# Scan spacing of twelve steps, and a reordered first job, in a one-core hybrid decoder layer

## The chip, the core and the metric

The kernel runs on one core of a Trainium2 chip. TensorE (PE in the profile) multiplies matrices, VectorE (DVE) and ScalarE (ACT) do elementwise work, GpSimd (POOL) some elementwise work and DMA issues, and SyncE (SP) issues DMAs. The metric is device time in microseconds, the median of several executions. The three runs shown lie within 0.45 us of each other; the profile shows one execution.

## The reference

One layer with parallel head groups is applied to a prompt (16 learned meta tokens and 256 prompt tokens) and to a sample group of 8 sequences of 4 tokens: T = 304 columns in all. D_MODEL is 2048, the feed-forward width 5632, and all data are fp32.

```python
xp = _layernorm(jnp.concatenate([meta, x_prompt], axis=1), ln0_g, ln0_b)
xs = _layernorm(x_sample, ln0_g, ln0_b)
...
proj = x @ w_in                       # q, zf, v, g (8 heads x 128 each), gate_b, gate_c, xin
...
# per head and chunk of 64 tokens
a = jnp.einsum('bhtk,bhsk->bhts', qc * jnp.exp(b - b_mid), kc * jnp.exp(b_mid - b))
o = einsum(where(causal, a, 0), vc) + einsum(qc * jnp.exp(b), S)
S = jnp.exp(b_last) * S + einsum(kc * jnp.exp(b_last - b), vc)
...
o = o * lax.rsqrt(jnp.mean(jnp.square(o), axis=-1, keepdims=True) + RMS_EPS)
o_a = o * gnorm_g * jax.nn.silu(g)
y_b = gate_b * conv(gate_c * xin)
mix = jnp.concatenate([o_a, y_b], axis=-1) @ w_o
h = _layernorm(ALPHA * x + mix, ln1_g, ln1_b)
ff = (jax.nn.silu(h @ w_gate) * (h @ w_up)) @ w_down
out = _layernorm(ALPHA * h + ff, ln2_g, ln2_b)
```

The scan state and the last convolution inputs are outputs too.

## The kernel before, in words

**Products.** Activations stand transposed, features on the 128 partitions and tokens along the free dimension. A product of fp32 precision is made of three: both operands are split into a high part rounded to the PE's fp32r type and a low rest (`hi`, `lo` of a weight, `mh`, `ml` or `xh`, `xl` of an activation), and hi*high, hi*low and lo*high are accumulated. Weights come in pieces of 4 blocks of 128 rows by 256 columns (`raw`, 512 KB, issued by SP). ACT casts a piece to `hi` and DVE subtracts to get `lo`, a few pieces ahead of PE.

**Jobs and steps.** The work is a row of jobs (`run_job`): a job makes 256 output rows in two PSUM banks from all blocks k of the contraction, six products to a block. After each block `tick()` is called: this is one step. Everything else is written as generators in named lanes (`side`), and each lane goes on to its next `yield` at a step; `yield n` skips n steps. So the order in which the small work stands in the program is counted in steps of six products. A list scheduler may then move instructions of an engine, except those issued through `vec`, `act`, `pool`, `pe` and `sync`, which keep their written order. Each engine runs its own queue strictly in order (PE's weight loads apart).

**Jobs in order.** Four jobs (z, v, q, gate) for each of four pairs of heads, with three convolution jobs each (cb, xb, gbb) between and after them, then eight jobs for w_o, then the feed-forward in two halves (gate, up, down).

**Scans.** `scan_head(h, ...)` runs eight times in one lane, one after the other. It transposes v (`vtb`) at its first step; DVE and ACT form the decays (`c`, `b`, `el`, `eb`), the scaled keys `kp` and `kd`; POOL multiplies the old state (`sn`, line 641); 15 steps after `vtb` PE transposes the keys (`ktb`, lines 661 to 663), two steps later it makes the scores (`ab`), and 15 steps after `ktb` the output (`ob`). Then it starts the lane `gated` for this head and ends with `yield GAP`, so the next head's scan starts GAP steps after `ob`. `gated` squares `ob` four steps after it, lets PE average (`nb`) two steps later, and about four steps after that begins eight DVE operations of 128x288 (`c<-nb`, `w<-eq`, ... `ml<-eq,mh`), the last of which makes this head's rows of the mixer input. Heads 2p and 2p+1 wait for the four jobs of pair p; the first scan also waits for step DEFER = 96.

**The first job.** The input rows are in three tiles `xts` (128, 128 and 48 rows, 2048 columns), loaded in four column chunks c of 512. `centre` subtracts a rough mean from a chunk, `turn(k)` transposes block k on PE (`xT`), `settle(k)` makes `mh` (ACT) and `ml` (DVE) of it. The first job (`zb`, `first_rhs`) runs on these centred but unnormalised rows; the LayerNorm's mean and scale are applied afterwards to its output. The statistics of tiles 0 and 1 come from `bn_stats` on DVE; those of tile 2 from two passes of ACT over all 2048 columns (`row_sums`, `junk`). `rstd_tok` turns them into `xr` and `xn`, PE broadcasts those into `rb`, and after `rb` the transposes `pb` and `bufT` of parameter rows stand, then the job vT. `idle_product` multiplies the identity with itself, at the front, to no end but PE activity. `lower_bounds` forms `loglb` and its kin from `pb`.

```python
        yield GAP                                    # last line of scan_head
...
            if k in BN_AT:
                b = BN_AT.index(k)
                row_stats(b % 2, b // 2)
            if k in (9, 10):
                next(sums)
```

Of the kernel before, what the change touches and what calls it, by code (L numbers as in the profile page):

```python
# [9 lines left out]
F32 = mybir.dt.float32  # L10
# [3 lines left out]
ALU = mybir.AluOpType  # L14

P = 128
# [25 lines left out]
DEFER = 96  # L42
BN_AT = (1, 3, 5, 6, 7, 9, 10, 11)
WARM = 3
LAG = 4
GAP = 8
NX = 7
# [16 lines left out]
def hybrid_step(ctx: ExitStack, tc: tile.TileContext, io):  # L64
# [166 lines left out]

    load_rows(pool, prow0, 0, ("ln0_g",))
    ident = const.tile([P, P], F32, name="ident")
    make_identity(nc, ident)

    def pcol(name, i):
# [106 lines left out]
    with s0x:  # L343
# [3 lines left out]
        bns = [x0p.tile([P, NXC, 6], F32, name=f"bn{i}") for i in range(2)]  # L347
        s2t = x0p.tile([P, 3], F32, name="s2t")
        prows = x0p.tile([NP1, P], F32, name="prows")
# [31 lines left out]
        def idle_product(n):  # L381
            pe.matmul(warm[:, : n * P], ident, ident.unsqueeze(1).broadcast_to([P, n, P]), start=True, stop=True)

        for _ in range(WARM):
            idle_product(4)
        idle_product(2)

# [8 lines left out]
        def centre(i, c, eng):  # L396
            n = rows[i]
            x, m = xts[i][:n, c * XC : (c + 1) * XC], cen[:n, i : i + 1]
            if eng is act:
                eng.activation(out=x, in_=x, func=AF.Identity, bias=m)  # L400
            else:
                eng.tensor_scalar(out=x, in0=x, scalar1=m, scalar2=None, op0=ALU.add)
# [15 lines left out]

        def row_sums():

            n = rows[2]
            x2, m2, s2 = xts[2][:n], mv[:n, 2], s2t[:n]
            junk = x0p.tile([n, D], F32, name="junk")
            act.activation(out=junk, in_=x2, func=AF.Identity, accum_out=s2[:, 0:1])
            vec.tensor_scalar(out=m2[:, 0:1], in0=s2[:, 0:1], scalar1=1.0 / D, scalar2=None, op0=ALU.mult)
            vec.tensor_scalar(out=s2[:, 2:3], in0=s2[:, 0:1], scalar1=-1.0 / D, scalar2=None, op0=ALU.mult)
            yield
            act.activation(out=junk, in_=x2, func=AF.Square, bias=s2[:, 2:3], accum_out=s2[:, 1:2])
            vec.tensor_scalar(out=m2[:, 1:2], in0=s2[:, 1:2], scalar1=1.0 / D, scalar2=None, op0=ALU.mult)
            yield  # L430

        row_centre(0)
        centre(0, 0, vec)
        row_centre(2)
        centre(2, 0, act)
        row_centre(1)
        centre(1, 0, vec)
        pb = bank("pb", "main")
        pe.transpose(pb[:, :NP0], prow0, ident[:NP0, :NP0])
        vec.tensor_copy(out=pvec[:, :NP0], in_=pb[:, :NP0])  # L440
        turn(0)
        turn(1)
        idle_product(2)
        settle(0)
# [5 lines left out]
        for _ in first_split:  # L450
            pass
        sums = row_sums()
        stats = []
# [5 lines left out]
        def first_rhs(k):  # L459
            c, i = divmod(k, 4)  # L460
            if i == 0:
                for j in (2, 3):
                    turn(k + j)
                for j in (2, 3):
                    settle(k + j)
                if c + 1 < NXC:
                    for j, eng in ((2, act), (0, vec), (1, act if c else vec)):
                        centre(j, c + 1, eng)
                if k == 0:
                    load_rows(pool, prows, NP0, ("b_f", "lb_param", "gnorm_g", "ln1_g", "ln1_b"))  # L470
                    pool.dma_start(out=crows, in_=io["conv_w"][0].rearrange("j (a b) -> (j a) b", b=P))
                    pool.dma_start(out=brow, in_=io["state_conv"][0].rearrange("b j c -> (b j) c"))
            if i == 2:
                split_next()
                if k + 2 < NB:
                    for j in (2, 3):
                        turn(k + j)
                    for j in (2, 3):
                        settle(k + j)
            if k in BN_AT:  # L480
                b = BN_AT.index(k)
                row_stats(b % 2, b // 2)
            if k in (9, 10):
                next(sums)
            if k == 13:
                for j in range(2):
                    vec.bn_aggr(out=mv[:, j], in_=bns[j])
                stats.extend(rstd_tok(x0p, mv, P, 3, "x"))
            return mixh[:, k], mixl[:, k]

        first_job = run_job(first_rhs, T + 2, "zb", pe)

        rb = [bank("rb") for _ in range(2)]
        for b, src in zip(rb, stats):
            for i in range(3):
                pe.matmul(b[:, i * P : i * P + rows[i]], src[:, i : i + 1].broadcast_to([P, P]), ident[:, : rows[i]],
                          start=True, stop=True)
        pb = bank("pb")
# [6 lines left out]
        for i in range(H):  # L505
            nc.tensor.transpose(bb_[:, i * 2 * DB : (i + 1) * 2 * DB], brow[:, i * P : (i + 1) * P], ident[: 2 * DB, : 2 * DB])
        nc.vector.tensor_copy(out=bufT, in_=bb_[:, : H * 2 * DB].rearrange("p (i b j) -> p i b j", b=DB, j=2))

    s2 = ExitStack()
# [794 lines left out]
```

## Time and profile before

| | |
|---|---|
| median of 3 runs | 1414.9 us (1414.69 to 1415.14) |
| profiled execution, its own time | 1415.39 us |
| its span in the trace | 1413.7 us |
| PE busy | 1388.5 us (98%) |
| DVE, ACT, POOL busy | 868.1, 604.7, 106.4 us |
| mean granted PE clock | 0.994 |
| weights and all else read from HBM | 222.34 MB |

The time of an execution has 1.7 us outside the span. PE is busy for nearly the whole span, so what is not PE's own work is found by listing where PE idles, not by the shares of the other engines. The granted clock is the share of the full PE clock that the chip allows in a stretch.

### The profile page before, as it was taken

The page shows a single profiled execution, that of the slowest core. Times are in us where ns is not written, and L with a number is a line of the kernel's source. Part 1 is how long each engine was busy: PE and PEld are TensorE (multiplying, and loading weights), DVE is VectorE, ACT ScalarE, POOL GpSimd, SP SyncE. Part 2 cuts the span into 40 slices and gives each one's busy share as a digit, 9 for nine tenths or more (in the row PEclk, how much of TensorE's full clock was granted, in tenths as well). Part 3 has the DMA queues.
Part 4 walks back from the last instruction along what each step waited for, and adds up shares of the span by engine and source line. Part 5 has one row for each costly group of instructions (what it writes and reads, how often), then busy time and mean ns, then how long its engine had stood idle before and what let it go on. Part 6 is the DMA issues. An engine that isn't in the chain of part 4 may idle for free.

```text
span 1413.7 us, 25159 instructions
## 1 busy us (share of the span) xinstructions
PE 1388.5 (98%) x10333; PEld 1369.3 (97%) x10333; DVE 868.1 (61%) x1431; ACT 604.7 (43%) x880; POOL 106.4 (8%) x165
## 2 busy tenths in 40 slices
PE   8999999999999999999999999999999999999996
PEld 6999999999999999999999999999999999999995
DVE  7996877786676787966444444443444444465544
ACT  6775445545443444434333333333333333343330
POOL 4000111111010332000000000000000000020000
PEclk9999999999999999999999999999999999999997
DMA  7746555455545555555555545556555555565541
GB/s 213 229 150 186 152 165 166 136 158 167 167 144 162 158 158 164 167 170 165 167 167 165 165 149 164 165 166 179 168 167 168 167 164 164 165 195 165 156 128 68
DMA packets 224660, 231.14 MB, mean 164 GB/s; under 512 B 7964, under 2 KB 219784, under 8 KB 224410
## 3 DMA queue, kind: packets, MB, share of 16 engines
q1 hardware_dynamic: 220688, 218.03, 50.5%
q0 software_dynamic: 3552, 11.12, 2.7%
q8 instruction: 81, 1.33, 0.4%
q10 hardware_dynamic: 304, 0.37, 0.1%
q14 instruction: 35, 0.29, 0.1%
HBM read 222.34 MB, written 7.15 MB: 162 GB/s over the span
## 4 chain that ended last, share of the span: by engine, by line
PE 90%; DVE 7%; ACT 2%; issue 1%; POOL 0%; DVEq 0%; POOLq 0%; ACTq 0%
PE u L201 7%; PE g L201 7%; PE wd L203 7%; PE g L202 7%; PE u L202 7%; PE wd L202 7%; PE g L203 7%; PE u L203 7%; PE wd L201 7%; PE wo L202 2%; PE wo L201 2%; PE wo L203 2%; DVE lo L79 1%; PE sg L201 1%; PE vT L203 1%; PE sg L202 1%
## 5 line engine op out<-in xcount | busy, mean ns | idle before, releaser
L79 DVE TENSOR_TENSOR lo<-raw,hi 128x1024 fp32r<-128x1024 f32 (+1 forms) x408 | 498.6, 1224 | 468.5 <-ACT hi L78 467.8
L78 ACT CAST hi<-raw 128x1024 fp32r<-128x1024 f32 (+1 forms) x408 | 420.7, 1032 | 614.7 <-PE u L202 162.6
L202 PE MATMUL wd<-al,hi 128*128 128x288 f32 x704 | 207.9, 295 | 0.0
L201 PE MATMUL wd<-ah,hi 128*128 128x288 f32 x704 | 207.8, 295 | 0.0
L203 PE MATMUL wd<-ah,lo 128*128 128x288 f32 x704 | 207.8, 295 | 0.0
L201 PE MATMUL g<-ygh,hi 128*128 128x288 f32 (+1 forms) x452 | 134.0, 296 | 0.0
L202 PE MATMUL g<-ygl,hi 128*128 128x288 f32 (+1 forms) x452 | 134.0, 296 | 0.0
L202 PE MATMUL u<-ygl,hi 128*128 128x288 f32 (+1 forms) x452 | 133.9, 296 | 0.0
L201 PE MATMUL u<-ygh,hi 128*128 128x288 f32 (+1 forms) x452 | 133.8, 296 | 0.0
L203 PE MATMUL g<-ygh,lo 128*128 128x288 f32 (+1 forms) x452 | 133.6, 296 | 0.0
L203 PE MATMUL u<-ygh,lo 128*128 128x288 f32 (+1 forms) x452 | 133.6, 296 | 0.0
L202 PEld LDWEIGHTS wd<-al,hi 128*128 128x128 f32 x704 | 132.3, 188 | 0.0
L203 PEld LDWEIGHTS wd<-ah,lo 128*128 128x128 f32 x704 | 132.2, 188 | 0.0
L201 PEld LDWEIGHTS wd<-ah,hi 128*128 128x128 f32 x704 | 132.1, 188 | 0.1
L203 PEld LDWEIGHTS u<-ygh,lo 128*128 128x128 f32 x452 | 85.4, 189 | 0.0
L203 PEld LDWEIGHTS g<-ygh,lo 128*128 128x128 f32 x452 | 85.3, 189 | 0.0
L201 PEld LDWEIGHTS g<-ygh,hi 128*128 128x128 f32 x452 | 85.3, 189 | 0.1
L202 PEld LDWEIGHTS g<-ygl,hi 128*128 128x128 f32 x452 | 85.3, 189 | 0.1
L201 PEld LDWEIGHTS u<-ygh,hi 128*128 128x128 f32 x452 | 85.3, 189 | 0.0
L202 PEld LDWEIGHTS u<-ygl,hi 128*128 128x128 f32 x452 | 85.3, 189 | 0.0
L203 PE MATMUL wo<-mh,lo 128*128 128x288 f32 x256 | 75.8, 296 | 0.0
L202 PE MATMUL wo<-ml,hi 128*128 128x288 f32 x256 | 75.8, 296 | 0.0
(461 smaller groups left out, 3206.1 us busy)
## 6 DMA issues: line engine op xcount, KB each, us to landing
raw<-in_w_in SPq DMA_DIRECT2D x111, 512.0 KB, 3.7
raw<-in_w_gate SPq DMA_DIRECT2D x88, 512.0 KB, 3.6
raw<-in_w_up SPq DMA_DIRECT2D x88, 512.0 KB, 3.6
raw<-in_w_down SPq DMA_DIRECT2D x79, 512.0 KB, 3.6
raw<-in_w_o SPq DMA_DIRECT2D x32, 512.0 KB, 3.7
s<-in_state_hgrn POOLq DMA_DIRECT2D x8, 512.0 KB, 5.7
out<-sn POOLq DMA_DIRECT2D x8, 512.0 KB, 4.6
raw<-in_w_down SPq DMA_DIRECT2D x15, 256.0 KB, 2.8
```

The lines of the kernel that those rows point to most:

```text
L78: a.copy(out=hi, in_=src)
L79: v.tensor_tensor(out=lo, in0=src, in1=hi.bitcast(F32), op=ALU.subtract)
L201: eng.matmul(o, hi[:, i % kb, cs], xh, start=(i == 0), stop=False)
L202: eng.matmul(o, hi[:, i % kb, cs], xl, start=False, stop=False)
L203: eng.matmul(o, lo[:, i % kb, cs], xh, start=False, stop=(i == nk - 1))
```

## The change

GAP goes from 8 to 12: each scan starts twelve steps after the `ob` of the one before. In the first job the second tile's statistics are gathered while it is centred: the ACT centring of tile 2 also writes its sum for the chunk (`accum_out`), four ACT passes over 512 columns add the squares (`row_squares` at k = 5, 7, 9, 11), and `row_moments` combines these on DVE at k = 13; the two passes over 2048 columns go. Chunks 2 and 3 of tile 0 are centred by POOL instead of DVE. The eight `bn_stats` move to later k. Of the idle products, 3 of 512 columns and 2 of 256 become 3 of 512; the one small transpose `pb` of the front moves between them. On POOL the DMA of `ln0_g` comes after the identity instead of before it, and the parameter rows' DMAs come at k = 4 instead of k = 0, behind POOL's first centring. The transposes `pb` and `bufT` behind the first job, and `lower_bounds`, are written ahead of `rb`.

```diff
--- before.py
+++ after.py
@@ -40,10 +40,11 @@
 NXC = 4
 NRAW = 8
 DEFER = 96
-BN_AT = (1, 3, 5, 6, 7, 9, 10, 11)
-WARM = 3
+BN_AT = (3, 5, 6, 7, 9, 10, 11, 12)
+SQ_AT = (5, 7, 9, 11)
+WARM = 2
 LAG = 4
-GAP = 8
+GAP = 12
 NX = 7
 RAW = 4
 ORDER = (("head", 0), ("head", 1), ("conv", 0), ("head", 2), ("conv", 1), ("head", 3), ("conv", 2), ("conv", 3))
@@ -229,9 +230,9 @@
             off[name] = row
             row += n
 
-    load_rows(pool, prow0, 0, ("ln0_g",))
     ident = const.tile([P, P], F32, name="ident")
     make_identity(nc, ident)
+    load_rows(pool, prow0, 0, ("ln0_g",))
 
     def pcol(name, i):
         return pvec[:, off[name] + i : off[name] + i + 1]
@@ -345,7 +346,7 @@
 
         mv = x0p.tile([P, 3, 2], F32, name="mv")
         bns = [x0p.tile([P, NXC, 6], F32, name=f"bn{i}") for i in range(2)]
-        s2t = x0p.tile([P, 3], F32, name="s2t")
+        s2t = x0p.tile([P, 2, NXC], F32, name="s2t")
         prows = x0p.tile([NP1, P], F32, name="prows")
         crows = x0p.tile([3 * H, P], F32, name="crows")
         xts = [x0p.tile([P, D], F32, name=f"xt{i}") for i in range(3)]
@@ -383,7 +384,9 @@
 
         for _ in range(WARM):
             idle_product(4)
-        idle_product(2)
+        pb = bank("pb", "main")
+        pe.transpose(pb[:, :NP0], prow0, ident[:NP0, :NP0])
+        idle_product(4)
 
 
         cen = x0p.tile([P, 3], F32, name="cen")
@@ -397,7 +400,7 @@
             n = rows[i]
             x, m = xts[i][:n, c * XC : (c + 1) * XC], cen[:n, i : i + 1]
             if eng is act:
-                eng.activation(out=x, in_=x, func=AF.Identity, bias=m)
+                eng.activation(out=x, in_=x, func=AF.Identity, bias=m, **({"accum_out": s2t[:n, 0, c : c + 1]} if i == 2 else {}))
             else:
                 eng.tensor_scalar(out=x, in0=x, scalar1=m, scalar2=None, op0=ALU.add)
 
@@ -416,31 +419,32 @@
             vec.scalar_tensor_tensor(out=mixl[:, k, :T], in0=b, scalar=g, in1=mixh[:, k, :T].bitcast(F32),
                                      op0=ALU.mult, op1=ALU.subtract)
 
-        def row_sums():
-
+        junk = x0p.tile([rows[2], XC], F32, name="junk")
+
+        def row_squares(c):
             n = rows[2]
-            x2, m2, s2 = xts[2][:n], mv[:n, 2], s2t[:n]
-            junk = x0p.tile([n, D], F32, name="junk")
-            act.activation(out=junk, in_=x2, func=AF.Identity, accum_out=s2[:, 0:1])
-            vec.tensor_scalar(out=m2[:, 0:1], in0=s2[:, 0:1], scalar1=1.0 / D, scalar2=None, op0=ALU.mult)
-            vec.tensor_scalar(out=s2[:, 2:3], in0=s2[:, 0:1], scalar1=-1.0 / D, scalar2=None, op0=ALU.mult)
-            yield
-            act.activation(out=junk, in_=x2, func=AF.Square, bias=s2[:, 2:3], accum_out=s2[:, 1:2])
-            vec.tensor_scalar(out=m2[:, 1:2], in0=s2[:, 1:2], scalar1=1.0 / D, scalar2=None, op0=ALU.mult)
-            yield
+            act.activation(out=junk, in_=xts[2][:n, c * XC : (c + 1) * XC], func=AF.Square, accum_out=s2t[:n, 1, c : c + 1])
+
+        def row_moments():
+
+            for i in range(2):
+                vec.bn_aggr(out=mv[:, i], in_=bns[i])
+            n = rows[2]
+            m2, sums = mv[:n, 2], x0p.tile([P, 3], F32, name="sums")[:n]
+            vec.tensor_reduce(out=sums[:, :2], in_=s2t[:n], op=ALU.add, axis=mybir.AxisListType.X)
+            vec.tensor_scalar(out=m2, in0=sums[:, :2], scalar1=1.0 / D, scalar2=None, op0=ALU.mult)
+            vec.tensor_scalar(out=sums[:, 2:], in0=m2[:, 0:1], scalar1=-1.0, scalar2=None, op0=ALU.mult)
+            vec.scalar_tensor_tensor(out=m2[:, 1:2], in0=m2[:, 0:1], scalar=sums[:, 2:], in1=m2[:, 1:2], op0=ALU.mult, op1=ALU.add)
 
         row_centre(0)
         centre(0, 0, vec)
         row_centre(2)
         centre(2, 0, act)
+        vec.tensor_copy(out=pvec[:, :NP0], in_=pb[:, :NP0])
         row_centre(1)
         centre(1, 0, vec)
-        pb = bank("pb", "main")
-        pe.transpose(pb[:, :NP0], prow0, ident[:NP0, :NP0])
-        vec.tensor_copy(out=pvec[:, :NP0], in_=pb[:, :NP0])
         turn(0)
         turn(1)
-        idle_product(2)
         settle(0)
         gb0 = pvec[:, :NP0].rearrange("p (a b) -> p b a", b=NB)
         split(gb0, mixh[:, :, T:], mixl[:, :, T:], vec, act)
@@ -449,7 +453,6 @@
         settle(1)
         for _ in first_split:
             pass
-        sums = row_sums()
         stats = []
 
         def row_stats(i, c):
@@ -464,9 +467,9 @@
                 for j in (2, 3):
                     settle(k + j)
                 if c + 1 < NXC:
-                    for j, eng in ((2, act), (0, vec), (1, act if c else vec)):
+                    for j, eng in ((2, act), (0, pool), (1, act)) if c else ((2, act), (0, vec), (1, vec)):
                         centre(j, c + 1, eng)
-                if k == 0:
+                if k == 4:
                     load_rows(pool, prows, NP0, ("b_f", "lb_param", "gnorm_g", "ln1_g", "ln1_b"))
                     pool.dma_start(out=crows, in_=io["conv_w"][0].rearrange("j (a b) -> (j a) b", b=P))
                     pool.dma_start(out=brow, in_=io["state_conv"][0].rearrange("b j c -> (b j) c"))
@@ -480,21 +483,14 @@
             if k in BN_AT:
                 b = BN_AT.index(k)
                 row_stats(b % 2, b // 2)
-            if k in (9, 10):
-                next(sums)
+            if k in SQ_AT:
+                row_squares(SQ_AT.index(k))
             if k == 13:
-                for j in range(2):
-                    vec.bn_aggr(out=mv[:, j], in_=bns[j])
+                row_moments()
                 stats.extend(rstd_tok(x0p, mv, P, 3, "x"))
             return mixh[:, k], mixl[:, k]
 
         first_job = run_job(first_rhs, T + 2, "zb", pe)
-
-        rb = [bank("rb") for _ in range(2)]
-        for b, src in zip(rb, stats):
-            for i in range(3):
-                pe.matmul(b[:, i * P : i * P + rows[i]], src[:, i : i + 1].broadcast_to([P, P]), ident[:, : rows[i]],
-                          start=True, stop=True)
         pb = bank("pb")
         nc.tensor.transpose(pb[:, :NP1], prows, ident[:NP1, :NP1])
         nc.tensor.transpose(pb[:, P : P + 3 * H], crows, ident[: 3 * H, : 3 * H])
@@ -505,6 +501,12 @@
         for i in range(H):
             nc.tensor.transpose(bb_[:, i * 2 * DB : (i + 1) * 2 * DB], brow[:, i * P : (i + 1) * P], ident[: 2 * DB, : 2 * DB])
         nc.vector.tensor_copy(out=bufT, in_=bb_[:, : H * 2 * DB].rearrange("p (i b j) -> p i b j", b=DB, j=2))
+
+        rb = [bank("rb") for _ in range(2)]
+        for b, src in zip(rb, stats):
+            for i in range(3):
+                pe.matmul(b[:, i * P : i * P + rows[i]], src[:, i : i + 1].broadcast_to([P, P]), ident[:, : rows[i]],
+                          start=True, stop=True)
 
     s2 = ExitStack()
     sp = s2.enter_context(tc.tile_pool(name="sp", bufs=1))
```

What this does to the queues is shown at three places.

PE, the start of the program, before (`warm` is an idle product, `xt_110`, `xt_112`, `xt_111` are the tiles 0, 2 and 1):

```order
L60 MATMUL warm<-ident 128x512 x3
L60 MATMUL warm<-ident 128x256
L60 MATMUL pb<-ident,prow_70 128x32
L60 MATMUL xT<-ident,xt_110 128x128
L60 MATMUL xT<-ident,xt_112 128x48
L60 MATMUL xT<-ident,xt_111 128x128
```

and in the changed kernel:

```order
L61 MATMUL warm<-ident 128x512 x2
L61 MATMUL pb<-ident,prow_70 128x32
L61 MATMUL warm<-ident 128x512
L61 MATMUL xT<-ident,xt_110 128x128
L61 MATMUL xT<-ident,xt_112 128x48
L61 MATMUL xT<-ident,xt_111 128x128
```

The small transpose now stands between the idle products, and one idle product less lies ahead of the first `xT`; the 256-column one that followed six of the `xT` is gone as well.

DVE, the end of the first job's statistics, before (`bn`, `mv`: statistics; `xv`, `xt`, `xr`, `xn` here: variance, temporary, scale and shift of the rows):

```order
L60 BN_AGGR mv<-bn_105 128x2
L60 BN_AGGR mv<-bn_106 128x2
L60 TENSOR_SCALAR xv<-mv 128x3
L60 TENSOR_TENSOR xt<-xr 128x3
L60 TENSOR_TENSOR xt<-xt,xv 128x3
L60 TENSOR_SCALAR xt<-xt 128x3
L60 TENSOR_TENSOR xr<-xr,xt 128x3
L60 SCALAR_TENSOR_TENSOR xn<-mv,xr 128x3
L60 TENSOR_TENSOR lo<-raw,hi 128x1024
L501 COPY pvec<-pb 128x64
```

and in the changed kernel, from just behind the first `bn_aggr` to the variance `xv`; eight more rows follow up to `xr`, four of them (`es`, `loglb`, `nloglb`, `logom`) of `lower_bounds`:

```order
L497 COPY pvec<-pb 128x64
L61 BN_AGGR mv<-bn_106 128x2
L61 TENSOR_REDUCE sums<-s2t 48x2
L498 COPY cvec<-pb 128x24
L61 TENSOR_SCALAR mv<-sums 48x2
L299 TENSOR_TENSOR lmx<-pvec 128x8
L503 COPY bufT<-bufT 128x128
L61 TENSOR_SCALAR sums<-mv 48x1
L301 TENSOR_TENSOR dd<-pvec,lmx 128x8
L302 TENSOR_TENSOR dd<-pvec,lmx 128x8
L61 SCALAR_TENSOR_TENSOR mv<-mv,sums 48x1
L61 TENSOR_SCALAR xv<-mv 128x3
```

The parameter copies and the lower bounds, which stood behind `xn`, are now mixed into the chain that ends in `xr`; a last `bn_stats` also stands behind the last `ml` where none stood.

DVE, the fourth gate and the fifth scan (head 4), before (`c<-nb`, `w<-eq`, `eq<-...`: the gate of head 3; `vt`, `vbd`, `c<-z`, `k`: the scan of head 4; `lo`: weight pieces):

```order
L742 TENSOR_SCALAR c<-nb 128x288
L589 COPY vt<-vtb 128x256
L79 TENSOR_TENSOR lo<-raw,hi 128x1024
L314 TENSOR_TENSOR w_3195<-eq 128x288
L315 TENSOR_TENSOR w_3195<-w_3195,c 128x288
L604 TENSOR_TENSOR vbd<-vsb,bmask 128x1024
L585 SCALAR_TENSOR_TENSOR c<-z,w_3157 128x304
L316 TENSOR_SCALAR w_3195<-w_3195 128x288
L586 TENSOR_SCALAR c<-c,logom 128x304
L317 TENSOR_TENSOR eq<-eq,w_3195 128x288
L594 TENSOR_TENSOR k<-c,z 128x304
L751 TENSOR_TENSOR eq<-ob,eq 128x288
```

and in the changed kernel:

```order
L744 TENSOR_SCALAR c<-nb 128x288
L315 TENSOR_TENSOR w_3275<-eq 128x288
L316 TENSOR_TENSOR w_3275<-w_3275,c 128x288
L317 TENSOR_SCALAR w_3275<-w_3275 128x288
L80 TENSOR_TENSOR lo<-raw,hi 128x1024
L318 TENSOR_TENSOR eq<-eq,w_3275 128x288
L587 SCALAR_TENSOR_TENSOR c<-z,w_3289 128x304
L753 TENSOR_TENSOR eq<-ob,eq 128x288
L588 TENSOR_SCALAR c<-c,logom 128x304
L754 TENSOR_TENSOR eq<-eq,sg 128x288
L591 COPY vt<-vtb 128x256
L596 TENSOR_TENSOR k<-c,z 128x304
```

The copy `vt`, which cannot run before PE has transposed v, stood one row behind the gate's first row and now stands behind nearly all of the gate. From `w<-eq` to the last `kd` row there are two `lo` rows in this scan before and three now.

## Prediction

> **What bounds the kernel now.** I read the page's first lines, then a table of stages, then what PE waited for, then the timeline at the largest wait. First the page:
>
> ```profile
> span 1413.7 us, 25159 instructions
> PE 1388.5 (98%) x10333; PEld 1369.3 (97%) x10333; DVE 868.1 (61%) x1431; ACT 604.7 (43%) x880; POOL 106.4 (8%) x165
> ```
>
> PE is idle for 25.2 us in all (1413.7 - 1388.5). The stages say where. The columns are the stretch, its length, busy time of PE, of PE's weight loads, DVE, ACT, POOL, then the granted clock, the DMA share and GB/s:
>
> ```profile
> 0.00:10.36 10.36, 7.76 (x24) 3.88 (x24) 6.30 (x15) 3.83 (x8) 8.16 (x32) 1.00 0.83 219
> 10.36:34.50 24.14, 21.32 (x155) 19.73 (x155) 20.57 (x48) 17.58 (x31) 7.46 (x25) 1.00 0.77 211
> ...
> 100.00:420.00 320.00, 311.85 (x2333) 302.81 (x2332) 242.54 (x504) 156.84 (x276) 40.39 (x46) 0.99 0.53 160
> 420.00:1390.00 970.00, 970.00 (x7302) 969.06 (x7301) 522.23 (x701) 373.16 (x464) 45.90 (x56) 1.00 0.53 162
> 1390.00:1413.70 23.70, 12.18 (x57) 8.68 (x56) 12.16 (x37) 1.22 (x4) 0.00 (x0) 0.69 0.29 100
> ```
>
> From 420 to 1390 us PE never idles: 7302 products take 970.00 us, 0.1328 us each, so a step of six is 0.80 us. The change touches the first 34.5 us (PE idle for 2.60 + 2.82 us) and the scans, where PE idles for 320.00 - 311.85 = 8.15 us. Next, what PE waited for from 100 to 560 us (total, times, longest):
>
> ```profile
> PE ktb L661 <- DVE kp L630: 5.5, 5, 2.1
> PE ktb L662 <- DVE kd L638: 1.7, 5, 1.0
> PE ab L668 <- DVE eq L643: 0.9, 1, 0.9
> ```
>
> All 8.1 us are waits of the transposes of keys (and one score product) for DVE. The largest, in head 4, on the timeline (start, duration; idle before in brackets):
>
> ```profile
> 252.11 0.45 DVE L742 TENSOR_SCALAR c<-nb 128x288 f32<-128x288 f32 x1
> 252.96 0.27 PE L570 MATMUL vtb<-ident,vT 128*16 128x128 f32 x1
> 253.27 0.42 DVE L589 COPY vt<-vtb 128x256 f32<-128x256 f32 x1 [0.71 <-PE vtb L570]
> ...
> 264.38 2.10 POOL L641 TENSOR_TENSOR sn<-s,eb 128x1024 f32<-128x1024 f32 x1 [21.80 <-ACT eb L612]
> 264.62 1.91 DVE L622 TENSOR_TENSOR w<-b 128x32 f32<-128x32 f32 x1
> 267.31 0.28 DVE L630 TENSOR_TENSOR kp<-kp,eb 128x128 f32<-128x128 f32 x1
> ...
> 267.65 0.44 PE L661 MATMUL ktb<-ident,kp 128*128 128x128 f32 x2 [2.08 <-DVE kp L630]
> ```
>
> DVE runs without a break from 253.27 to kp's end at 267.59, and PE wants kp at 267.65 - 2.08 = 265.57, which is 12.6 us (fifteen steps) behind `vtb`. In that time DVE must do the gate of head 3 as well. The 1.91 us row is an oddity: the row ahead of it in the trace, of the same 128x32 shape, takes 0.19. It starts under POOL's 2.10 us `sn` and ends with it; one DVE row does so in each of the eight scans.
>
> The wait has an echo in the clock:
>
> ```profile
> 262.10:265.50 3.40, 3.40 (x26) 3.23 (x24) 3.40 (x10) 1.85 (x3) 1.12 (x1) 1.00 0.83 250
> 265.50:269.00 3.50, 1.42 (x12) 1.33 (x12) 3.50 (x14) 2.28 (x6) 0.98 (x1) 0.99 0.14 47
> 269.00:272.40 3.40, 3.40 (x17) 3.40 (x17) 2.48 (x5) 1.39 (x4) 0.00 (x0) 0.50 0.27 70
> 272.40:275.80 3.40, 3.40 (x29) 2.82 (x29) 1.53 (x5) 0.25 (x1) 0.54 (x1) 1.00 0.80 236
> 227.00:230.40 3.40, 1.91 (x14) 1.42 (x13) 3.40 (x13) 1.91 (x7) 1.27 (x1) 1.00 0.50 154
> ```
>
> After the 2.08 us gap the clock was 0.50 for 3.4 us, and 17 products ran where 26 and 29 ran on either side: half of 3.4, 1.7 us, were lost. The last row is head 3, where PE idled for 1.49 us (3.40 - 1.91) and the clock stayed at 1.00.
>
> **The change, part by part.**
>
> *GAP.* Four steps more between `ob` and the next `vtb` are 4 x 0.80 = 3.19 us. The gate's start is tied to its own `ob`, so `c<-nb`, now 0.85 us ahead of `vtb` (252.96 - 252.11), will come about 4.0 ahead. The quoted order shows what that does: between `c<-nb` and `vt` stand six more gate rows, one `lo` and two scan rows, some 5.3 us, so `vt` runs about 1.3 us behind `vtb` (0.31 now). Behind `vt`, up to kp, are left one gate row and the scan's own, with two `lo`; by start-to-start times in the trace these are 9.9 us with the 1.73 us that `sn` costs. So kp is ready 1.3 + 9.9 = 11.2 us behind `vtb`, against 12.6: 1.4 us early instead of 2.1 late. What speaks against a full gain is the count of `lo` rows from `w<-eq` to `kd`: 2, 3, 2, 2, 2 before in heads 2, 3, 4, 5, 7, and 4, 3, 3, 3, 3 after. Their group from 100 to 420 us (busy time, mean ns of one, idle time before them):
>
> ```profile
> L79 DVE TENSOR_TENSOR lo<-raw,hi 128x1024 fp32r<-128x1024 f32 x83 | 101.0, 1222 | 50.4 <-ACT hi L78 50.0
> ```
>
> One is 1.22, or 1.15 from start to start, and may itself wait for ACT's `hi`. I leave 1.0 us of the 8.15 standing (bounds 0 and 5.15, one `lo` in each of the five heads: 5 x 1.15 = 5.75, less what they have in hand; I take the low side because the margin just worked out already holds its extra `lo`): **-7.15**. Behind it nothing is late: six gaps of 3.19 do not add up, since every second head waits for its pair's jobs too; by the order head 7's `vtb` stands only 23 of PE's rows, about four steps, later. The last row of its gate and the first use of the mixer input now:
>
> ```profile
> 438.58 0.45 DVE L79 TENSOR_TENSOR ml<-eq,mh 128x288 fp32r<-128x288 f32 x1
> ...
> L201 PEld LDWEIGHTS wo<-mh,hi x256: 187/188/193, 443.1 to 546.3; 128*128 128x128 f32 x128
> ```
>
> 439.03 + 3.19 = 442.2, still ahead of 443.1.
>
> *The clock.* Without a gap over 2 us the stretch at 269 goes: **-1.7** (0 if a gap like that survives).
>
> *`sn`* stays and blocks one DVE row of a scan as now. The Trainium skill, page "SBUF — State Buffer", section "Who interferes with whom", says that a DVE instruction with two SBUF inputs contends with a GpSimd one that reads SBUF, and that the first to issue locks the shared port pair for its whole length. The trace agrees (1.91 us beside 2.10). By that rule POOL's two new centrings could each hold a DVE `ml` or `lo` for their full length, up to twice 1.05 us (half of `sn`'s length for half its columns), and not free DVE by the 0.96 us worked out below; the first job would be up to 1.1 us worse.
>
> *The first job.* Its rows:
>
> ```profile
> 1.32 0.64 POOL L60 DMA_DIRECT2D prow<-in_ln_g  x1 [0.80 <-POOLq L1292]
> 2.60 5.01 PE L60 MATMUL warm<-ident 128*128 128x512 f32 x8 [2.60 <-POOL ident masks.py:199]
> 8.89 0.60 PE L60 MATMUL warm<-ident 128*128 128x256 f32 x2
> 12.17 1.05 ACT L60 CAST hi<-raw 128x1024 fp32r<-128x1024 f32 x1
> 21.69 1.33 ACT L60 ACTIVATE xt<-xt,cen 48x512 f32<-48x512 f32 x2
> 22.92 1.90 ACT L60 ACTIVATE junk<-xt 48x2048 f32<-48x2048 f32 x1
> 23.15 0.48 DVE L60 TENSOR_SCALAR xt<-xt,cen 128x512 f32<-128x512 f32 x1
> 26.55 2.01 ACT L60 ACTIVATE junk<-xt,s2t 48x2048 f32<-48x2048 f32 x1
> 28.75 0.67 DVE L60 BATCH_NORM_STATS2 bn<-xt 128x6 f32<-128x512 f32 x1
> 30.23 0.37 DVE L60 BATCH_NORM_AGGREGATE mv<-bn 128x2 f32<-128x24 f32 x2
> 31.91 0.16 DVE L60 TENSOR_TENSOR xr<-xr,xt 128x3 f32<-128x3 f32 x1
> 32.22 0.84 PE L60 MATMUL rb<-ident,xr 128*128 128x128 f32 x6 [0.46 <-DVE xr L60]
> 33.66 0.27 PE L499 MATMUL pb<-ident,prows 64*128 64x64 f32 x1
> 34.51 0.41 PE L201 MATMUL vT<-mh,hi 128*128 128x306 f32 x1
> ```
>
> Front: the identity comes 0.64 earlier (the issue at 1.32 goes behind it), and of the idle products 0.60 us fall away. That would be worth 0 to 1.24, but the next thing PE needs is a weight's `hi`, which starts at 12.17 whatever PE does; I keep 0.45, the third nearest the row that ends last. Shorter idle work costs nothing while the clock is 1.00, as here from 10 us on.
>
> ACT: the passes of 1.90 and 2.01 become four of 512 columns at 0.67 (half of the 21.69 row, `accum_out` free), so 1.2 us less on the engine that is busy 12.45 of 13.51 us between 15.94 and 29.45:
>
> ```profile
> 15.94:29.45 13.51, 12.07 (x88) 11.29 (x86) 11.28 (x23) 12.45 (x20) 2.50 (x5) 1.00 0.88 252
> ```
>
> I take 0.9 of it (0 to 1.2), since some of ACT's order is fixed by landings. POOL's two centrings free 2 x 0.48 on DVE, which is not the later engine there: 0 (bounds -0.96 and +1.1). The parameter rows' DMAs move on POOL's queue behind its first centring, to k = 4 of 16, and `pb` wants them at about 30: hidden by eleven blocks of the job. So the last `ml` ends near 30.23 + 0.07 - 1.35 = 28.95.
>
> Behind it DVE now has a `bn_stats` (0.67), two aggregates (0.37), and about fourteen small rows, six of them parameter copies and lower bounds, where the trace has 1.77 us from the last `ml` to `xr`'s end. At 0.15 to 0.2 each: 0.67 + 0.37 + 2.8 is about 3.9 us, so `rb` near 33.0 against 32.22 (+0.8). But `pb` and `bufT`, which took PE 0.85 us (33.66 to 34.51) between `rb` and vT, are done in the wait ahead of `rb`. vT: 34.51 + 0.8 - 0.85, that is **0.0** (bounds -2.0, if the tail overlaps the last products, and +1.0, at 0.25 a row).
>
> **Sum.** 1415.39 - 7.15 - 1.7 + 0.0 = 1406.5. The profiled execution is 0.5 above the median of 1414.9, so **1406.0**. Nothing after 420 us changes.
>
> **Rivals.** A change of 0.2% (2.8 us) is about what can be told from none; faster means below 1412.1.
>
> A (as summed): 1406.0, chance 0.46.
>
> B: as A, but the gap ahead of `rb` sets off a half-clock stretch. PE has only `pb` and `bufT` between the first job's end near 29.5 and `rb` at 33.0, idling for about 2.4 us against 0.46 now. For it: 2.08 us did so in head 4. Against it: 1.49 did not, and the small transposes break the gap. Price 1.7: 1407.7, chance 0.26. By the Trainium skill, page "TensorE: Matmul & The Clock Gate", section "Why this matters for your kernels", only gaps over about 3 us bring the clock down, and A would hold; the 2.08 us in this trace were less than that, so I go by the trace.
>
> C: half of the waits stay (4.1 in place of the 1.0 above, +3.1), the 269 stretch goes, and the first job ends at its late bound (+1.0): 1406.0 + 4.1 = 1410.1, chance 0.13. For it: the row of `ktb` on kd above, five waits of its own that one early kp does not remove.
>
> D: the lead of four steps is eaten by the additional `lo` rows and the waits are as before: 1414.9, chance 0.08. Against it: `sn` and the scan's own rows alone fit in the time.
>
> E, slower: the `lo` rows that slide into the stretch behind `vt` each wait for `hi`. The 83 of them waited 50.4 us for it, though none in the busy stretch of head 4. That is 0.6 each. Then the later `vt` eats half of what the four steps gain (4.1 of 8.15 left), and five more rows of 1.15 + 0.6 cost 8.75: 4.65 more than before. Gaps like head 3's 1.49 grow past 2 us in two more heads, two stretches of 1.7: 1414.9 + 4.65 + 3.4 = 1423. It decides where the time in hand of a head, 1.4 us as worked out, is under 1.75. Chance 0.07.
>
> **How the numbers follow.** A, B and C are faster (0.85, of which I give 0.02 to no change, for C with a bad first job); D is no change; E slower. The range runs from 1403.0 (A with the full 8.15 and 2.0 from the first job) to 1411.0 (C with 0.9 more); D and E, 0.15, lie outside.
>
> **What would show it.** Right: no row of `ktb` among PE's waits from 100 to 560; clock 1.00 in all of 100 to 420, PE busy over 318 of 320 us; vT within 1 us of 34.5 with `rb`'s wait near 2. B shows as 0.50 behind `rb`. Wrong: `ktb` still waits behind kp with a `lo` that waits for `hi` just ahead of it; or the last `ml` of the first job not earlier than 30 us, which would put vT past 35.5.

## The result

The changed kernel takes 1406.09 us (median of 4 runs, 1405.59 to 1406.49) against 1414.8 (4 runs): a ratio of 0.9938, 95% interval 0.9921 to 0.9955. The forecast was 1406.0. The total is right; two of its terms are not, and their errors cancel.

The page of the changed kernel first, then its stages (the columns as above), then what PE waited for from 100 to 560 us:

```profile
span 1404.6 us, 25157 instructions
PE 1387.1 (99%) x10329; PEld 1368.6 (97%) x10329; DVE 865.5 (62%) x1430; ACT 602.7 (43%) x888; POOL 110.4 (8%) x167
```

```profile
0.00:10.36 10.36, 7.67 (x14) 3.00 (x14) 5.10 (x12) 2.75 (x6) 8.35 (x33) 1.00 0.78 210
10.36:34.50 24.14, 22.50 (x150) 20.44 (x150) 21.14 (x57) 17.84 (x43) 9.84 (x27) 1.00 0.77 215
...
100.00:420.00 320.00, 318.64 (x2409) 311.27 (x2409) 246.78 (x513) 160.81 (x282) 41.02 (x47) 1.00 0.55 167
```

```profile
PE ktb L663 <- DVE kp L632: 1.0, 2, 0.8
PE ktb L664 <- DVE kd L640: 0.3, 2, 0.2
```

PE now idles for 1.36 us of the 320 instead of 8.15, and eleven waits are four, in heads 1 and 7. Head 4, where the largest wait was:

```profile
257.52 0.46 DVE L744 TENSOR_SCALAR c<-nb 128x288 f32<-128x288 f32 x1
...
262.37 0.27 PE L572 MATMUL vtb<-ident,vT 128*16 128x128 f32 x1
...
263.09 0.41 DVE L591 COPY vt<-vtb 128x256 f32<-128x256 f32 x1
...
272.26 0.28 DVE L632 TENSOR_TENSOR kp<-kp,eb 128x128 f32<-128x128 f32 x1
...
274.55 0.38 PE L663 MATMUL ktb<-ident,kp 128*128 128x128 f32 x2
```

The gate begins 4.85 us ahead of `vtb`, `vt` is 0.72 us behind it, and kp is done at 272.54, 2.0 us before PE takes it.

The end of the first job, where the forecast was less good:

```profile
29.89 0.96 DVE L61 SCALAR_TENSOR_TENSOR ml<-xT,pvec,mh 128x304 fp32r<-128x304 f32 x2
...
34.02 0.16 DVE L61 TENSOR_TENSOR xr<-xr,xt 128x3 f32<-128x3 f32 x1
...
34.32 0.84 PE L61 MATMUL rb<-ident,xr 128*128 128x128 f32 x6 [1.36 <-DVE xr L61]
...
35.66 0.38 PE L202 MATMUL vT<-mh,hi 128*128 128x306 f32 x1
```

The last `ml` ends at 30.85 (28.95 was forecast, 30.30 before), the chain to `xr` takes 3.33 us (3.9 forecast), and vT starts at 35.66, 1.15 us later than before.

### The profile page after: what moved, and what is told of

Same layout as the page of the kernel before. It is cut to its first block, busy times and chain, and to the rows that moved or that the text cites. A ratio compares the mean times of both kernels' runs of the same rounds, so it can differ in the third digit from the quotient of the medians.

```text
span 1404.6 us, 25157 instructions
## 1 busy us (share of the span) xinstructions
PE 1387.1 (99%) x10329; PEld 1368.6 (97%) x10329; DVE 865.5 (62%) x1430; ACT 602.7 (43%) x888; POOL 110.4 (8%) x167
## 3 DMA queue, kind: packets, MB, share of 16 engines
q8 instruction: 81, 1.33, 0.4%
HBM read 222.34 MB, written 7.15 MB: 163 GB/s over the span
## 4 chain that ended last, share of the span: by engine, by line
PE 94%; DVE 3%; ACT 1%; issue 0%; DMA 0%; DVEq 0%; POOL 0%; POOLq 0%; ACTq 0%
PE g L202 7%; PE u L202 7%; PE wd L204 7%; PE g L203 7%; PE u L203 7%; PE wd L203 7%; PE g L204 7%; PE u L204 7%; PE wd L202 7%; PE wo L203 2%; PE wo L202 2%; PE wo L204 2%; PE vT L202 1%; PE vT L204 1%; PE vT L203 1%; PE sg L202 1%
## 5 line engine op out<-in xcount | busy, mean ns | idle before, releaser
L202 PE MATMUL wo<-mh,hi 128*128 128x288 f32 x256 | 75.8, 296 | 0.0
```

Source lines behind the costliest of these rows:

```text
L202: eng.matmul(o, hi[:, i % kb, cs], xh, start=(i == 0), stop=False)
```

## The experiments

Three moments of each traced execution split its time: the end of the first job's last `ml`, the start of vT, and the way from vT to the first w_o product, in which all scans lie. Behind that w_o product all kernels take 970.4 to 970.6 us, the two with GAP = 16 take 971.3. In `pb_back_dve` PE took vT's first products ahead of `rb`, so its last two columns do not compare with the others.

| kernel | median, us | last ml ends | vT starts | vT to w_o |
|---|---|---|---|---|
| before | 1414.8 | 30.30 | 34.51 | 408.74 |
| changed | 1406.09 | 30.85 | 35.65 | 398.34 |
| gap12 | 1405.9 | 31.57 | 35.77 | 398.74 |
| gap12_again | 1406.61 | 31.49 | 35.69 | 398.74 |
| after_again | 1405.73 | 30.43 | 35.24 | 398.34 |
| first_only | 1413.98 | 30.65 | 35.45 | 406.77 |
| old_tail | 1409.02 | 30.55 | 36.80 | 400.50 |
| old_front | 1404.72 | 28.80 | 33.59 | 398.39 |
| pb_back | 1403.61 | 28.35 | 33.16 | 398.34 |
| pb_back_dve | 1404.64 | 30.96 | 34.15 | 399.84 |
| old_front_gap16 | 1403.37 | 29.62 | 34.42 | 395.94 |
| pb_back_gap16 | 1402.27 | 28.52 | 33.33 | 395.94 |
| sn_late | 1405.45 | 30.68 | 34.89 | 397.92 |

**One part alone.** `gap12` is the kernel before with only the spacing:

```diff
-GAP = 8
+GAP = 12
```

> The kernel before with GAP = 12 and nothing else. Theory 1 (from the trace of the changed kernel: from the first vT product to the first w_o product it took 398.34 us instead of 408.74, while vT itself starts 1.14 us later): the spacing alone is worth 10.4 us, so 1414.9 - 10.4 = 1404.5, and this kernel is faster than the changed one by about 1.2 us. Theory 2 (the prediction's sum): the spacing is worth 8.85 us and the first job nothing, so 1406.0, the same as the changed kernel.

Measured: 1405.9 us (5 runs), ratio to before 0.9934 (0.9922 to 0.9947). The spacing alone is the whole gain, as theory 2 had it. The way from vT to w_o fell nearly as theory 1 said, but the same old first job that started vT at 34.51 in the traced execution of before started it at 35.77 here. So one execution does not tell what the new first job is worth. What scatters it can be seen in part. Before, `sn_late`, `gap12_again` and `gap12` have the same first job; in their traces the clock rises at 6.14, 6.88, 7.97 and 6.79 us, zb's first product starts at 10.36, 10.73, 11.27 and 10.69, and in `gap12` ACT also waits 1.52 us for the DMA of a weight piece.

`first_only` is the changed kernel with `GAP = 8`.

> The changed kernel with GAP back at 8: the first job alone. Theory 1: vT starts near 35.65 us instead of 34.51 and nothing behind it gains, so 1414.9 + 1.1 = 1416.0. Theory 2: the first job is worth 0, 1414.9. A third reading, that the waits of the scans went because the first job shifted them against the clock's windows and the weight loads, expects part of the 8.8 us here, below 1412.

Measured: 1413.98 us (11 runs, 1412.04 to 1417.03), ratio 0.9995 (0.9986 to 1.0004): no change. Why its runs spread over 5 us is not known. It has exactly the waits of before:

```profile
PE ktb L663 <- DVE kp L632: 5.5, 5, 2.1
PE ktb L664 <- DVE kd L640: 1.7, 5, 1.0
PE ab L670 <- DVE eq L645: 0.9, 1, 0.9
```

and yet its way from vT to w_o is 1.97 us shorter. Of this, 0.40 goes with the first job: with GAP = 12 the way is 398.74 with the old one (`gap12`, `gap12_again`) and 398.34 with the new one. The other 1.57 go with the clock. Head 4's wait of about 2.1 us in the two traces, first before, then `first_only` (two and three windows of the grid; the eighth number is the clock):

```profile
265.54:268.96 3.42, 1.33 (x12) 1.29 (x12) 3.42 (x14) 2.24 (x6) 0.94 (x1) 1.00 0.14 44
268.96:272.37 3.41, 3.41 (x18) 3.41 (x17) 2.51 (x4) 1.43 (x4) 0.00 (x0) 0.50 0.26 67
```

```profile
263.50:266.91 3.41, 2.58 (x20) 2.35 (x18) 3.41 (x7) 1.78 (x3) 2.01 (x1) 1.00 0.65 198
266.91:270.33 3.42, 2.16 (x17) 2.15 (x18) 3.42 (x15) 3.09 (x9) 0.09 (x1) 1.00 0.02 5
270.33:273.74 3.41, 3.41 (x31) 2.83 (x31) 2.46 (x6) 0.57 (x1) 0.00 (x0) 1.00 0.49 149
```

All changes of the clock in a trace lie on a grid of 3.41 us. Before, the whole gap fell into one window of it (PE busy for 1.33 of 3.42); in `first_only` it was split over two (2.58 and 2.16), and the clock stayed. So the stretch cost about 1.6 us here, and whether it comes depends on how the grid falls in that execution. How often it comes in the executions of before is not known. What the spacing saves without it is 406.77 - 398.34 = 8.43 us.

**The two first jobs side by side.**

> The changed kernel once more, beside the next one on the same chip. Theory 1 (the prediction's term for the first job, 0.0): the two are within 0.4 us of each other, and vT's start, which was 35.65, 35.77, 35.45 us in kernels with and without the new first job and 34.51 in the profiled execution of before, scatters by about 1 us from execution to execution with the same code. Theory 2 (the first job as changed costs 1.1 us): this one is slower by 1.1.

> The kernel before with GAP = 12 once more: the old first job. Theory 1: the time of the changed kernel within 0.4 us, and vT between 34.5 and 35.8. Theory 2: 1.1 us below it, with vT at 34.5.

Measured: 1405.73 (1405.27 to 1406.86) and 1406.61 (1405.25 to 1406.84). With the earlier runs, nine of the changed kernel have a mean of 1406.03 and ten of the old first job with GAP = 12 one of 1406.15. The new first job is worth 0.1 us, which is nothing that these runs can tell. The medians here lie 0.9 apart, more than the 0.4 that theory 1 allowed, in overlapping ranges; theory 2 asked for the opposite sign.

**The front.** `old_front` puts back what the change did ahead of the first `xT`:

```diff
-WARM = 2
+WARM = 3
...
-        pb = bank("pb", "main")
-        pe.transpose(pb[:, :NP0], prow0, ident[:NP0, :NP0])
-        idle_product(4)
+        idle_product(2)
...
         centre(1, 0, vec)
+        pb = bank("pb", "main")
+        pe.transpose(pb[:, :NP0], prow0, ident[:NP0, :NP0])
+        vec.tensor_copy(out=pvec[:, :NP0], in_=pb[:, :NP0])
         turn(0)
         turn(1)
+        idle_product(2)
```

with `load_rows` for `ln0_g` ahead of the identity again. `pb_back` moves only `pb` and its copy back; the identity stays first and the idle products stay three.

> The changed kernel with the front of before: ln0_g loaded ahead of the identity, three idle products of 512 columns and two of 256, pb behind the centrings; statistics, POOL's centrings and the tail as changed. Theory 1: the front is what cost time (the first zb product at 11.98 us instead of 10.35, pb waiting 1.26 us on PE's queue for its DMA, the clock at 0.5 until 14.48 us instead of 6.13); with the old one zb starts near 10.4, the last ml ends 1 to 1.6 us earlier than 30.85, and the time is 1404.5 to 1405.1. Theory 2 (landings set the first job, the front's start does not matter): 1406.1, the last ml within 0.3 us of 30.85.

> The changed kernel with the small transpose pb moved back behind all three idle products and the centrings; the identity stays ahead of ln0_g's DMA, and the number of idle products stays 3. Theory 1 (pb's wait for its DMA cuts the run of idle products, so no window of 3.41 us is full and the clock stays at 0.5 until 14.5 us): now the products run from 1.4 us without a cut, the clock rises by 8 us, zb starts near 10.3 and the time is near 1404.7, as with the whole old front. Theory 2 (it is the number of idle products that matters, 1536 columns end at about 6.5 us with nothing behind them until the first xT): the clock still rises only at about 14 us and the time is 1406.

Measured: 1404.72 (5 runs) and 1403.61 (4 runs, 1403.32 to 1405.66). Theory 1 holds in both, and the gain is larger than it said: the last `ml` ends at 28.80 and 28.35, and `pb_back` was to be near 1404.7. PE's front in the changed kernel and in `pb_back`:

```profile
1.43 3.78 PE L61 MATMUL warm<-ident 128*128 128x512 f32 x4 [1.43 <-POOL ident masks.py:199]
6.47 0.31 PE L61 MATMUL pb<-ident,prow 32*128 32x32 f32 x1 [1.26 <-DMA prow<-in_ln_g]
6.71 2.08 PE L61 MATMUL warm<-ident 128*128 128x512 f32 x2
8.58 3.75 PE L61 MATMUL xT<-ident,xt 128*128 128x128 f32 x12
```

```profile
1.43 5.49 PE L61 MATMUL warm<-ident 128*128 128x512 f32 x6 [1.43 <-POOL ident masks.py:199]
6.84 0.26 PE L61 MATMUL pb<-ident,prow 32*128 32x32 f32 x1
7.03 2.48 PE L61 MATMUL xT<-ident,xt 128*128 128x128 f32 x12
```

In the changed kernel `pb` stands on PE's queue while its DMA, now issued later, is under way; PE idles for 1.26 us, the granted clock rises only at 14.48 us, and twelve transposes take 3.75 us. (The clock column reads 1.00 ahead of that because the trace records no clock before its first change. The products show it: zb's start 0.25 us apart up to 14.4 and 0.14 behind.) In `pb_back` the idle products are not cut, the clock rises at 6.91, and they take 2.48. The first zb product starts at 9.26 instead of 11.99. In `after_again` the grid falls otherwise, with the same end: the clock rises at 4.85, is down again behind the window with `pb`'s wait (4.85 to 8.26), and stays down until 15.09. Of the traces with the new statistics, the five with the new front end the last `ml` at 30.28 (`clock_dose`) to 30.85, the four with uncut idle products and POOL's centrings at 28.35 to 29.62.

**The tail.** `old_tail` writes `pb`, `bufT` and `lower_bounds` behind `rb` again, as before.

> The changed kernel with pb, bufT and the lower bounds written behind rb again. In the changed kernel the chain from the last ml to xr took 3.33 us and rb to vT 1.33 (before: 1.77 and 2.30). Theory 1: the mixed-in rows and the wait for lse cost the chain about as much as PE gains, so the chain falls to about 2.4 us, rb to vT rises to 2.3, and the time is 1406.1 within 0.3. Rival: the mixed-in rows only fill idle time of DVE; then the chain keeps its 3.3 us and the time is 1407.1.

Measured: 1409.02, but the five runs spread from 1405.26 to 1409.65. The chain took 3.0 us and `rb` to vT 3.1, and the traced execution shows why:

```profile
31.33:34.75 3.42, 1.72 (x14) 1.50 (x13) 2.64 (x12) 1.34 (x3) 0.00 (x0) 1.00 0.00 0
34.75:38.16 3.41, 3.41 (x20) 3.16 (x19) 1.64 (x10) 0.81 (x5) 0.92 (x3) 0.50 0.52 156
38.16:41.57 3.41, 3.41 (x16) 3.41 (x15) 3.39 (x10) 3.31 (x7) 1.52 (x3) 0.50 0.60 159
```

The wait ahead of `rb` left PE 1.72 of 3.42 us in its window, and two windows of half clock followed, under transposes and the first products of vT. The lowest run lies where those of the changed kernel lie; its mean clock is 0.995, that of the four longer ones 0.992 to 0.993. Neither expectation fits the median; what the moved rows alone are worth stays open.

**What brings the clock down.** `clock_dose` puts twenty waits of graded length into w_o and the first gate and up jobs:

```diff
+        for n in (1, 2, 3, 4, 5) * 4:
+            pe.matmul(b, ident, ...)
+            for _ in range(n):
+                vec.tensor_reduce(out=stl, in_=b, op=ALU.add, ...)
+            pe.matmul(b2[:, :P], stl.broadcast_to([P, P]), ident, ...)
+            yield 11
```

> The changed kernel with twenty stalls of PE put into w_o and the first gate and up jobs: an idle product, then 1 to 5 DVE reductions of its bank, then a PE product that needs the last of them; the products of these jobs keep their written order. Time is not the point; the stalls add perhaps 40 us. It asks what brings the clock down. Theory 1 (from six traces: a window of 3.41 us on a fixed grid in which PE was busy for 0.39 or 0.50 of it was followed by half clock, one of 0.60 or more never): windows below about half busy are followed by 0.5 and those above 0.6 are not, so that the same idle time does it where it falls into one window and not where it is split over two. Theory 2 (the length of the gap decides, near 2 us): gaps of over 2 us do so wherever they fall, shorter ones never. Theory 3 (a gap must last a whole window, 3.4 us): only the longest do.

Measured: 1530.09 us in a single execution, so the stalls cost 124 us and not 40; PE waited 61.6 us for them, and the granted clock from 440 to 760 us was 0.88. Between 440 and 760 us, sixteen windows of the grid that were at full clock had PE busy for a share of 0.00 to 0.42, and all sixteen were followed by a window at 0.5; ten had 0.48 to 0.96, and none was. The rows next to the border, with the window behind each:

```profile
515.51:518.92 3.41, 1.64 (x8) 0.81 (x7) 3.41 (x4) 1.01 (x2) 3.04 (x3) 1.00 0.48 142
518.92:522.33 3.41, 0.00 (x0) 0.00 (x0) 3.31 (x5) 0.00 (x0) 0.00 (x0) 1.00 0.41 137
522.33:525.75 3.42, 2.40 (x10) 2.43 (x11) 0.84 (x2) 0.00 (x0) 0.00 (x0) 0.50 0.08 28
...
648.63:652.04 3.41, 1.43 (x7) 0.60 (x5) 3.41 (x7) 1.04 (x1) 0.00 (x0) 1.00 0.54 179
652.04:655.45 3.41, 0.62 (x3) 0.65 (x4) 3.41 (x9) 0.00 (x0) 0.00 (x0) 0.50 0.47 154
```

1.64 of 3.41 kept the clock, 1.43 did not. Theory 3 falls, since one gap of 2.07 us did it (busy 0.39). This run alone does not part theories 1 and 2: all its gaps of 2.07 us and more brought the clock down, and none of 1.60 and less did. Theory 2 falls by two other runs: a gap of 2.08 us that was split over two windows, 0.83 and 1.25, did nothing in `first_only`, and one of 1.70 within one window brought the clock down in `old_tail`. So theory 1 holds, but not its border: windows with 0.50 in `old_tail` and 0.60 in the front of `after_again` were followed by half clock, too. Where the border lies between 0.4 and 0.6, and whether it is the same for every kind of product, stays open.

**Why the scans were late.** `sn_late` leaves GAP at 8 and only keeps POOL from starting `sn` while DVE works towards kp:

```diff
-        nc.gpsimd.tensor_tensor(out=sn, in0=s0, in1=ebs.broadcast_to([P, DB, P]), op=ALU.mult)
...
         nc.vector.tensor_mul(out=ep, in0=ends[:, :, 0], in1=ends[:, :, 1])
+        ebe = sp.tile([P, DB, 1], F32, tag="ebe", name="ebe")
+        nc.vector.tensor_copy(out=ebe, in_=ebs)
+        nc.gpsimd.tensor_tensor(out=sn, in0=s0, in1=ebe.broadcast_to([P, DB, P]), op=ALU.mult)
```

> The kernel before, GAP = 8, with one row moved in the scan: POOL's sn product now reads a copy (128x8, on DVE) of the decays, written behind the scan's last DVE row, so it cannot start while DVE works towards kp. Theory 1 (DVE is late for ktb by up to 2.1 us, of which 1.7 is the one row that sn blocks; the twelve steps won only because they made up for that): kp comes 1.7 us earlier in every scan, head 4's gap falls from 2.1 to about 0.4 us and the others (1.3 and less) go, 7.8 us of 8.15, with 1 to 1.5 us more where PE starts again: 1406 or a little below, like GAP = 12. Theory 2 (sn's block is made up elsewhere, the lo rows behind it set kp): the waits fall by less than half, 1411 or more. A third possibility is that the block lands on eq or ek instead and PE waits at ab: then the ab row grows by 1.7 us a scan.

Measured: 1405.45 us (5 runs), ratio 0.9932 (0.9919 to 0.9944): theory 1. The row that took 1.91 us in head 4 takes 0.18. PE waits only twice in the scans, once for kp in head 4 and once at `ab`, there for less than before (0.5 us for 0.9), so the block did not move to `ab`, the third possibility:

```profile
PE ab L670 <- DVE eq L642: 0.5, 1, 0.5
PE ktb L663 <- DVE kp L630: 0.4, 1, 0.4
...
260.25 0.18 DVE L622 TENSOR_TENSOR w<-b 128x32 f32<-128x32 f32 x1
261.21 0.28 DVE L630 TENSOR_TENSOR kp<-kp,eb 128x128 f32<-128x128 f32 x1
...
261.55 0.44 PE L663 MATMUL ktb<-ident,kp 128*128 128x128 f32 x2 [0.36 <-DVE kp L630]
```

One row of POOL moved did as much as twelve steps between scans. The two were not run together.

**POOL's centrings.** `pb_back_dve` gives the last two chunks of tile 0 back to DVE.

> As pb_back, with the last two chunks of tile 0 centred by DVE again instead of POOL. The prediction put POOL's centrings at 0 with bounds of -0.96 (DVE freed) and +1.1 us (DVE blocked). In the trace they take 1.57 us each on POOL, and the lo beside the first one 1.59 instead of 1.22. Theory 1 (0): 1403.6 within 0.3. Theory 2 (they free DVE): 1404.3 or more here. Theory 3 (the block costs as much as it frees or more): 1403.3 or less.

Measured: 1404.64 (1403.50 to 1406.17) against 1403.61 (1403.32 to 1405.66): it leans to theory 2, but the ranges overlap and the two ran on different chips (0.9924 and 0.9918 of before on the same chip), so the sign is not settled. The trace leans the same way: from the second to the third cast of a weight piece (`hi`, 128x1024) it takes 6.35 us here, and 5.08 to 5.21 in the nine traces with POOL's centrings. It is the slowest execution of the five, though, and the first such cast waited 3.03 us for its DMA, so its last `ml`, at 30.96, is not the centrings' doing alone. The cost that was expected beside POOL, in the changed kernel, is there, and small:

```profile
15.33 1.57 POOL L61 TENSOR_SCALAR xt<-xt,cen 128x512 f32<-128x512 f32 x1 [1.25 <-DMA xt<-in_x_prompt]
...
15.49 1.59 DVE L61 TENSOR_TENSOR lo<-raw,hi 128x1024 fp32r<-128x1024 f32 x1 [0.75 <-ACT hi L61]
```

**Beyond both kernels.**

> The old front with GAP = 16: aimed below both kernels. With GAP = 12 two scans, heads 1 and 7, still wait (1.0 + 0.3 us of PE). Theory 1: four more steps take those away, and w_o is still not late, so 1404.7 - 1.3 = 1403.4 with no ktb row among PE's waits. Rival: the last gate now ends behind the first w_o product that needs it; then PE waits there and the time is over 1405.5.

> The version that the runs so far point to: pb behind the idle products (1403.6 with GAP = 12) and GAP = 16 (1.35 us less in the pair with the old front). If the two add up, 1402.3. If the early first job only shifts the waits, 1403.5.

Measured: 1403.37 (5 runs) and 1402.27 (4 runs, 1402.06 to 1403.28), both as expected; ratio of the second to before 0.991 (0.9897 to 0.9924). The list of PE's waits in the scans is empty for both; the stage of `pb_back_gap16`:

```profile
100.00:420.00 320.00, 319.92 (x2424) 313.35 (x2422) 246.67 (x518) 162.05 (x281) 39.59 (x50) 1.00 0.55 167
```

`pb_back_gap16` is 3.8 us below the changed kernel.

## Why the prediction was right, and where it was not

*GAP, -7.15.* The mechanism is shown: `gap12` has the gain alone, and head 4's kp went from 2.1 us late to 2.0 early (1.4 forecast). PE's idle time fell by 6.79, so the 1.0 left standing was close to the measured 1.36. But the way from vT to w_o fell by 8.43 without any help of the clock, 1.64 more than the idle time. The step that failed is to price a wait by PE's idle time alone. By an estimate from the rows, a product's bar is 0.30 us long and the next starts 0.13 later, so the first 0.17 us of each gap are counted as busy; seven gaps went, 1.2 us. The remaining 0.4 are not explained. `sn_late` has about the same surplus for each gap: nine went there, PE's idle time fell by 7.26 (319.11 - 311.85), and the way by 9.25 (406.77 + 0.40 for the old first job - 397.92), 2.0 more: 0.22 for each gap, against 0.23 here. With GAP = 16 the last 1.25 us of idle time went; the way to w_o fell by 2.40, of which 0.8 came back behind it, so that 1.6 were saved (1.35 by the medians).

*The clock, -1.7.* The stretch measured 1.57, but it is no fixed term of the kernel: it depends on the grid in each execution, and `first_only` had the same gap without it. The profiled execution of before had the stretch, and an early first job as well (vT at 34.51, against 34.9 to 35.8 in the three other executions of the same code); so it stood near the median by two accidents. By the medians the change gained 8.7 us, of which the spacing alone explains 8.43, so little is left for the clock. GAP came out 1.3 too small and the clock more than 1 too large; that the sum was met to 0.1 us is luck.

*The first job, 0.0.* Right as a sum (0.1 by the means), wrong in its parts. The last `ml` was to end 1.35 us earlier. With the old front it does: 28.80 and 29.62 against 30.30 to 31.57 in the four executions of the old first job. The new front takes it away: 30.28 to 30.85. The step that failed is the front: `pb` was costed without its DMA, which the change had moved behind the identity on POOL's queue, and the clock was taken as given, though the idle products raised it for good only in the traces where they run without a cut. That there are fewer of them did cost nothing: `pb_back` has as few. The order of `pb` ahead of the last idle product stood in the quoted rows, and the wait could be read from it. Nor does the `hi` at 12.17 start there "whatever PE does": in `first_only` it starts at 13.23, without a wait for its DMA. The chain to `xr` (3.33 for 3.9) and `rb` to vT (1.33, 0.97 less, for 0.85 less) were close. POOL's centrings, put at 0, may have gained about 1 us; that is not settled. `accum_out` was taken as free; each use has a row of its own:

```profile
19.18 0.19 ACT L61 ACTIVATION_READ_ACCUMULATOR xt<-xt,cen 48x1 f32 x1
```

*The rivals.* B did not come in the changed kernel: PE idled for 1.36 us ahead of `rb`, not 2.4, since zb's last product ended at 32.96, not 29.5 (PE still had the last blocks to do behind the last `ml`, 1.45 us of them before, too). In `old_tail`, with a little more idle time (1.70 us), it did come. The 1.49 us of head 3, which were held against B, are two gaps, 1.32 and 0.17, and the longer one lay across two windows of the grid (0.67 and 0.65). The Trainium skill, page "TensorE: Matmul & The Clock Gate", section "What's actually happening", has a free-running window of 3413 ns, which all traces here agree with; its advice in "Why this matters for your kernels", no gaps over about 3 us, does not hold here: waits of 1.70, 2.07 and 2.08 us were enough. C, D and E are excluded by the four waits that are left.

*Its own signs.* PE busy over 318 us (318.64) and the clock at 1.00 in the scans came. `ktb` did not leave the list of waits (1.0 and 0.3 us), and `rb`'s wait was 1.36 instead of about 2. Of the signs of being wrong the last one came: the last `ml` ends behind 30 us (30.85) and vT starts past 35.5 (35.66).

*`sn`.* The prediction left it as it was, as a fixed cost of 1.73 us in a scan. `sn_late` shows that it was the larger part of what made the scans late (1.73 of head 4's 2.08 us). The Trainium skill, page "SBUF — State Buffer", section "Who interferes with whom", names the mechanism, a lock of the shared port pair for a whole instruction; the traces agree for `sn` (1.91 us for a row of 0.18), while beside POOL's centring of 1.57 us a `lo` of 1.22 took 1.59, so only 0.37 us were lost there, and the lock did not hold for the whole instruction.

## What to carry to other kernels

Look for the one long row on a late engine before moving the work around it: a short DVE row that lasts as long as the POOL row beside it is worth as much as four steps of slack. Idle time of PE is not the whole price of a wait (0.2 us more for each gap here), and a half-clock stretch in one trace may be an accident of the grid: look whether a second kernel with the same gap has it. Before a wait-prone instruction is moved between products that keep the clock up, ask what it waits for.

## What was not expected of the hardware

The clock follows PE's busy share in windows of 3.41 us: 0.42 and less was followed by half clock in all sixteen windows of `clock_dose`, 0.48 and more in none of ten. Behind a window at half clock it rose again, in the same run, when PE had been busy for 0.88 or more of it (16 windows), and stayed down at 0.72 and less (7). Transposes seem to count for less. The window with 0.60 that lost the clock in `after_again` (busy 2.05 of 3.41 us, 4.85 to 8.26) had about a third of its busy time in transposes. Windows at half clock that were busy throughout stayed down where transposes filled 0.73 of them (the changed kernel, 7.65 to 11.07) or 0.40 (`old_tail`, 34.75 to 38.16), and the clock rose behind those with 0.27 (the changed kernel, 11.07 to 14.48) or 0.33 (`after_again`, 11.67 to 15.09). No run varied the transposes alone, so this is read from these five windows and not tested.
